# One packed sum for row and offset of an expert slot, index casts on GpSimd, and three expert blocks emitted behind the last head

## The chip, the cores and the metric

The kernel runs on one core of one Trainium2 chip. The metric is the device time of one execution in microseconds. Of the kernel before, three executions gave 1765.59, 1766.91 and 1767.95 us; the median is 1766.91 us. One further execution was profiled; it took 1767.14 us, of which the span from its first to its last instruction is 1765.3 us.

## The reference: what is computed

One layer of an encoder trunk over 512 tokens of 1024 channels, in float32. The first half (attention, a matrix-memory mixer, gates, an output projection) is not touched by the change. The second half is a layer of 16384 single-neuron experts, addressed by product keys, and a final RMSNorm:

```
q = (xb @ w_pq).reshape(PEER_BLOCK, PEER_HEADS, 2, D_KEY // 2)
s = einsum("thpd,hpnd->thpn", q, sub_keys)          # 8 heads, 2 halves, 128 keys
s_top, i_top = top_k(s, 16)
cand = s_top[:, :, 0, :, None] + s_top[:, :, 1, None, :]   # 16 x 16 sums
best, ci = top_k(cand.reshape(..., 256), 16)
i1 = take_along_axis(i_top[:, :, 0, :], ci // 16)
i2 = take_along_axis(i_top[:, :, 1, :], ci % 16)
e = i1 * 128 + i2
gate = softmax(best)
act = gelu(einsum("thkd,td->thk", u_exp[e], xb))
out = einsum("thk,thkd->td", gate * act, v_exp[e])
```

So each token has 8 x 16 = 128 slots, and each slot has a row i1, a column i2 and a gate.

## The kernel before

**Dense experts for three quarters of the tokens.** For the last 384 tokens the kernel doesn't gather: it multiplies the tokens with all 16384 rows of u, in 128 blocks of 128 experts (`hidden`: one load of 512 KB, a split of the weights into a high and a low part, 24 matmuls of 384 columns, one GELU), weights the result with a dense gate matrix, and multiplies with v (`output`). The first 128 tokens gather their rows (`gathered`).

**Split weights.** Every weight tile is split in two halves of 512 columns. `split` lets ScalarE copy a half into a rounded high part `whi` (L150), and VectorE or GpSimd subtract it for the low part `wlo` (L153); in the stages discussed here the halves go to VectorE, GpSimd, GpSimd in turn. Each product is then three matmuls, L163 to L165, and the second operand of L165 needs `wlo`.

**The scores stage.** `scores` runs over eight heads. For a head it projects two queries (`ps_pq`, 2 x 24 matmuls of 512 columns), multiplies with the keys (`ps_sc`), and takes the 16 best of 128 keys, with their places, for four token tiles and two halves (`top16`, L647 to L651 on VectorE). It then calls `select`:

- L656 casts the places of the keys from uint32 to float32 (`idx`), 128 elements a partition.
- Only 50 of the 256 sums can be among the best 16; they lie as a staircase: row a of the staircase has 16 // (a + 1) candidates and begins at `OFFS[a]`. GpSimd forms them (L660, L663), `top16` finds the best 16 and their positions, L668 casts these (`pf`).
- L670 and L671 form `dl`, the differences of neighbouring rows' key indices. L686 forms a mask m over 16 x 16: position >= OFFS[a]. The product m * dl, summed over a, is the key index of the slot's row (L687 on GpSimd, L688 on VectorE, written to `slots`). The product m * (length of the row before), summed over a, is where the row begins (L689 on GpSimd, L690 on VectorE); L691 subtracts it from the position, which gives the offset in the row. L692, L693 and L694 turn the offset into the column's key index.

After the eight heads `scores` forms the gates (L634 to L641).

**The build stage.** For each of three token tiles `build` transposes the slots (`ps_slT`, L739), forms one-hot matrices on three engines (L750, L760, L761, L764) and multiplies them into the dense gate matrix (`ps_g`, L766). It has 32 steps a tile, 96 in all, and stores the matrix to HBM (L772, on GpSimd's queue).

**What sets the order.** `front` is a generator that yields twice for a head, once behind the gates and once for a build step. The loop at L938 to L944 counts these yields with n, adds `RATE_S` = 1.0 to a counter for the first 16 and `RATE_B` = 0.15 for those behind, and emits one block of `hidden` (through `ahead`) whenever the counter reaches one; 40 blocks are to be emitted in this way, and what is left then is emitted in one go by `drive` (L945). This is the order in which instructions are written down. Their order on each engine is made from it when the program is built, by a planner that runs the program in a model of its own and lets an engine take up something later in the text where what comes first isn't ready in that model. On the chip each engine then keeps its order and waits.

Of the kernel before, what the change touches and what calls it, by code (L numbers as in the profile page):

```python
# [10 lines left out]
F32 = mybir.dt.float32  # L11
# [5 lines left out]
ALU = mybir.AluOpType  # L17
AX = mybir.AxisListType
# [3 lines left out]
P = 128  # L22
# [8 lines left out]
TOPK = 16  # L31
STAIR = [TOPK // (a + 1) for a in range(TOPK)]
OFFS = [sum(STAIR[:a]) for a in range(TOPK)]
NC50 = sum(STAIR)
TB = 32
EG = 4
GG = 8
# [9 lines left out]
ADA_AT, ADA_N = 8, 2  # L47
OAP, OAD, TWO = 6, 16, 6
ACT_N, ACT_D = 2, 2
RATE_S, RATE_B, RATE_V = 1.0, 0.15, 2.5  # L50
WST, WB = 4, 5

LANES_A = lambda nc: [nc.vector]
# [3 lines left out]
C_BADA, C_G1, C_G2, C_CW, C_CB, C_MG, C_BG, C_OFF, C_DOFF, C_SEQ = 0, 48, 56, 64, 96, 104, 108, 112, 128, 144  # L57
# [17 lines left out]
def drive(*gens):  # L75
    for _ in weave(*gens):
        pass
# [3 lines left out]
def tile_block(  # L81
# [19 lines left out]
    nc = tc.nc  # L101
# [8 lines left out]
    def bank(tag, name):  # L110
        return psum.tile([P, 512], F32, tag=tag, name=name, bufs=4 if tag == "acc" else 2)
# [13 lines left out]
    cst = cpool.tile([P, C_N], F32, name="cst")  # L125
# [76 lines left out]
    x2d = dram.tile([4, P, D], F32, name="x2d")  # L202
    gd = dram.tile([S // TB, P, P, TB], F32, name="gd")
    gtd = dram.tile([1, D], F32, name="gtd")
# [440 lines left out]
    def top16(vals, places, data):  # L645

        nc.vector.max(vals[:, :8], data)  # L647
        nc.vector.max_index(places[:, :8], vals[:, :8], data)  # L648
        nc.vector.match_replace(data, vals[:, :8], data, LOWEST)  # L649
        nc.vector.max(vals[:, 8:], data)  # L650
        nc.vector.max_index(places[:, 8:], vals[:, 8:], data)  # L651

    def select(cp, h, sv, i16, best, slots):

        idx = cp.tile([P, 4, 2, TOPK], F32, tag="idx", name="idx")
        nc.vector.tensor_copy(idx, i16)  # L656
        cand = cp.tile([P, 4, NC50], F32, tag="cand", name="cand", bufs=1)
        for a in range(8):
            nb = STAIR[a]
            nc.gpsimd.tensor_add(  # L660
                cand[:, :, OFFS[a] : OFFS[a] + nb], sv[:, :, 1, :nb], sv[:, :, 0, a : a + 1].broadcast_to([P, 4, nb])
            )
        nc.gpsimd.tensor_add(cand[:, :, OFFS[8] :], sv[:, :, 0, 8:], sv[:, :, 1, 0:1].broadcast_to([P, 4, 8]))  # L663
        pos = cp.tile([P, 4, TOPK], U32, tag="pos", name="pos")
        for i in range(4):
            top16(best[:, i, h], pos[:, i], cand[:, i])
        pf = cp.tile([P, 4, TOPK], F32, tag="pf", name="pf")
        nc.vector.tensor_copy(pf, pos)  # L668
        dl = cp.tile([P, 4, TOPK], F32, tag="dl", name="dl")
        nc.vector.tensor_copy(dl[:, :, 0:1], idx[:, :, 0, 0:1])  # L670
        nc.vector.tensor_sub(dl[:, :, 1:], idx[:, :, 0, 1:], idx[:, :, 0, :-1])  # L671
        of = cp.tile([P, 4, TOPK], F32, tag="of", name="of")
        shp = [P, 4, TOPK, TOPK]

        def bc(t):
            return t.unsqueeze(3).broadcast_to(shp)

        def bs(t):
            return t.unsqueeze(2).broadcast_to(shp)

        def bq(col):
            return cst[:, col : col + TOPK].unsqueeze(1).unsqueeze(1).broadcast_to(shp)

        m = cp.tile(shp, F32, tag="m4", name="m4", bufs=1)
        q = cp.tile(shp, F32, tag="q4", name="q4", bufs=1)
        nc.vector.tensor_tensor(out=m, in0=bc(pf), in1=bq(C_OFF), op=ALU.is_ge)  # L686
        nc.gpsimd.tensor_mul(q, m, bs(dl))  # L687
        nc.vector.tensor_reduce(slots[:, :, 0, h], q, axis=AX.X, op=ALU.add)  # L688
        nc.gpsimd.tensor_mul(m, m, bq(C_DOFF))  # L689
        nc.vector.tensor_reduce(of, m, axis=AX.X, op=ALU.add)  # L690
        nc.vector.tensor_sub(of, pf, of)  # L691
        nc.vector.tensor_tensor(out=m, in0=bc(of), in1=bq(C_SEQ), op=ALU.is_equal)  # L692
        nc.gpsimd.tensor_mul(m, m, bs(idx[:, :, 1, :]))  # L693
        nc.vector.tensor_reduce(slots[:, :, 1, h], m, axis=AX.X, op=ALU.add)  # L694
# [40 lines left out]
    def build(cp, i, slots):  # L735
# [7 lines left out]
        nc.scalar.mul(neg, sT[:, 1:, :], -1.0)  # L743
        for b in range(P // TB):
            st = cp.tile([P, P, TB], F32, tag="gst", name="gst", bufs=2)
            for t4 in range(TB // 4):
                ps = bank("gw"[t4 % 2], "ps_g")
                o4 = cp.tile([P, 4, P], F32, tag="two", name="o4", bufs=TWO)
                t0 = b * TB + t4 * 4
                mark = nc.vector.tensor_tensor(  # L750
# [3 lines left out]
                for tt in range(4):  # L754
                    t = b * TB + t4 * 4 + tt
                    oa = cp.tile([P, P], F32, tag="oap" if tt == 1 else "oad", name="oa", bufs=OAP if tt == 1 else OAD)
# [19 lines left out]
    def gather_side(cp):  # L776
        for i in range(NG):
            yield from gathered(cp, i)

    def front(sp, dp, h2T):  # L780
        yield from scores(sp, h2T)
        for i in range(NG, 4):
            yield from build(dp, i, state["slots"][:, i])
# [97 lines left out]
    def pool(name, bufs=2, side="left"):  # L881
        return tc.tile_pool(name=name, bufs=bufs, side=side, reuse_waits="tile")
# [45 lines left out]
    with pool("epool") as cp:  # L928
        h2T = state["h2T"]
        held = cp.tile([P, HOLD, ND], F32, name="held", bufs=1)  # L930
        state["slots"] = cp.tile([P, 4, 3, 8, TOPK], F32, name="slots", bufs=1)
        with pool("dpool") as dp, pool("upool") as up:
            gt2 = dp.tile([P, D], F32, tag="m4", name="gt2", bufs=1)
            to_rows(gt2, mod[:, 40:48], 1.0)
            nc.sync.dma_start(gtd, gt2[:1, :])
            main, side = front(dp, dp, h2T), ahead(up, h2T, held)
            lanes["now"] = LANES_F(nc)
            n, due = 0, 0.0  # L938
            for _ in main:
                n += 1  # L940
                due += RATE_S if n <= 16 else RATE_B
                while due >= 1.0:
                    due -= 1.0
                    next(side, None)  # L944
            drive((side, 1))  # L945
            lanes["now"] = LANES_V(nc)
        if stop == "u":
            return
        with pool("vpool") as vp, pool("rpool") as rp:
            gather = gather_side(rp)  # L950
            with tc.issue_after(state["marks"][MARK]):
                next(gather)
                next(gather)
            paced(output(rp, vp, h2T, held), gather, RATE_V)
            drive((gather, 1))


def layout(inputs):
# [23 lines left out]
    consts = np.zeros((P, C_N), np.float32)  # L982
# [6 lines left out]
    consts[:BH, C_BG] = f["b_igate"][0]  # L989
    consts[32 : 32 + BH, C_BG] = f["b_fgate"][0]  # L990
    consts[:, C_OFF : C_OFF + 16] = OFFS
    consts[:, C_DOFF : C_DOFF + 16] = [0] + STAIR[:-1]
    consts[:, C_SEQ : C_SEQ + 16] = np.arange(16)

    dist = 3 * P + np.arange(P)[:, None] - np.arange(512)[None, :]
    return {
# [31 lines left out]
```

## Time and profile before

| | |
|---|---|
| median of three executions | 1766.91 us (1765.59 to 1767.95) |
| the profiled execution | 1767.14 us |
| its span | 1765.3 us |
| TensorE matmul (PE) busy | 1705.3 us, 97% |
| VectorE (DVE) busy | 1380.5 us, 78% |
| GpSimd (POOL) busy | 832.6 us, 47% |
| ScalarE (ACT) busy | 806.3 us, 46% |
| mean DMA rate | 234 GB/s |

In a row of a group, the numbers behind the bar of the count are the busy time in us, the mean duration of one instruction in ns, and the time that its engine sat idle just before such instructions, with what ended it. In a row of a stretch of time stand the busy time of each engine with its count of instructions, the granted TensorE clock as a share of full speed, the busy share of the DMA engines and their rate. In a row of waits stand the total in us, the number of waits and the longest.

### The profile page before, as it was taken

To read this page: it belongs to the slowest core of one execution; us is meant where nothing else is said; L and a number is where in the kernel's file an instruction comes from. 1 tells how busy PE (TensorE), PEld (TensorE's weight loads), DVE (VectorE), ACT (ScalarE), POOL (GpSimd) and SP (SyncE) were. 2 spreads that over 40 slices of the span, in tenths; PEclk is the share of its full clock that TensorE was granted. 3 is DMA by queue.
4 is the path that set the end of the run, shared out by engine and by line. 5 is a ranking of instruction groups with operands and counts; after the bars stand their busy time and mean duration, and the time that the engine had idled before them with its cause. 6 is when DMAs were issued, how large, how long until landed. Compare 5 with 4: busy or idle time off the path is not lost.

```text
span 1765.3 us, 25467 instructions
## 1 busy us (share of the span) xinstructions
PE 1705.3 (97%) x8671; PEld 1486.5 (84%) x8671; DVE 1380.5 (78%) x2868; ACT 806.3 (46%) x1624; POOL 832.6 (47%) x692
## 2 busy tenths in 40 slices
PE   5999999999999897999999999999999999999997
PEld 4766678888798787999899999999999999998886
DVE  7557655675589998899477988899989898898445
ACT  4544545443543334998533443433434443434443
POOL 0000000000157676999455666677776677673221
PEclk9999999999999998999999999999999999999999
DMA  8423224563332333565998989989999989987653
GB/s 292 152 73 127 88 99 140 186 227 100 111 104 89 104 101 135 204 255 233 343 367 322 358 308 344 352 324 342 348 326 351 353 303 351 350 293 282 228 194 107
DMA packets 129940, 413.35 MB, mean 234 GB/s; under 512 B 12049, under 2 KB 38801, under 8 KB 128274
## 3 DMA queue, kind: packets, MB, share of 16 engines
q1 hardware_dynamic: 91218, 252.33, 41.3%
q0 software_dynamic: 38592, 159.40, 24.1%
q8 instruction: 68, 1.11, 0.2%
q14 instruction: 62, 0.51, 0.1%
HBM read 376.03 MB, written 35.66 MB: 233 GB/s over the span
## 4 chain that ended last, share of the span: by engine, by line
PE 80%; DVE 13%; DMA 4%; issue 1%; POOL 1%; ACT 1%; SPq 0%; DVEq 0%; ACTq 0%
PE acc L165 10%; PE acc L164 10%; PE acc L163 10%; PE ps_act L165 8%; PE ps_act L163 8%; PE ps_act L164 8%; PE ps_g L766 4%; DVE wlo L153 2%; DMA wst<-in_w_ada 1%; PE ps_ya L361 1%; PE ps_s L341 1%; PE ps_qk L163 1%; DVE i L648 1%; PE ps_qk L165 1%; DVE sc L649 1%
## 5 line engine op out<-in xcount | busy, mean ns | idle before, releaser
L150 ACT CAST whi<-wst 128x512 fp32r<-128x512 f32 x408 | 252.1, 621 | 482.6 <-PE ps_act L164 279.6
L165 PE MATMUL ps_act<-h2T_hi,wlo 128*128 128x384 f32 x1024 | 348.3, 340 | 5.0 <-DVE wlo L153 4.0
L163 PE MATMUL ps_act<-h2T_hi,whi 128*128 128x384 f32 x1024 | 347.0, 339 | 0.0
L164 PE MATMUL ps_act<-h2T_lo,whi 128*128 128x384 f32 x1024 | 346.8, 339 | 0.0
L164 PE MATMUL acc<-wlo,ehi 128*128 128x512 f32 x768 | 299.1, 391 | 0.0
L163 PE MATMUL acc<-whi,ehi 128*128 128x512 f32 x768 | 293.3, 390 | 3.3 <-ACT whi L150 3.3
L165 PE MATMUL acc<-whi,elo 128*128 128x512 f32 x768 | 286.9, 391 | 0.0
L153 DVE TENSOR_TENSOR wlo<-wst,whi 128x512 fp32r<-128x512 f32 x275 | 207.0, 756 | 98.2 <-ACT whi L150 91.1
L153 POOL TENSOR_TENSOR wlo<-wst,whi 128x512 fp32r<-128x512 f32 x133 | 184.4, 1393 | 180.9 <-ACT whi L150 174.9
L150 ACT CAST whi<-vst 128x512 fp32r<-128x512 f32 x256 | 158.0, 620 | 181.2 <-PE acc L165 137.9
L724 POOL DMA_INDIRECT vr<-in_v_r,ei x128 | 168.6, 1317 | 84.5 <-DVE sum_v L730 65.9
L710 POOL DMA_INDIRECT ur<-in_u_r,ei x128 | 153.5, 1199 | 115.3 <-DVE junk L713 93.6
L153 POOL TENSOR_TENSOR wlo<-vst,whi 128x512 fp32r<-128x512 f32 x85 | 131.0, 1541 | 151.7 <-ACT whi L150 136.1
L165 PEld LDWEIGHTS ps_act<-h2T_hi,wlo 128*128 128x128 f32 x1024 | 193.8, 189 | 7.3 <-DVE wlo L153 5.2
L163 PEld LDWEIGHTS ps_act<-h2T_hi,whi 128*128 128x128 f32 x1024 | 194.0, 189 | 3.7
L164 PEld LDWEIGHTS ps_act<-h2T_lo,whi 128*128 128x128 f32 x1024 | 193.9, 189 | 3.7
L730 DVE SCALAR_TENSOR_TENSOR sum_v<-vr,act,sum_v 128x1024 f32<-128x1024 f32 x127 | 181.2, 1427 | 1.2 <-DMA vr<-in_v_r,ei 0.4
L713 DVE SCALAR_TENSOR_TENSOR junk<-ur,h 128x1024 bf16<-128x1024 f32 x128 | 170.9, 1335 | 0.9
L163 PEld LDWEIGHTS acc<-whi,ehi 128*128 128x128 f32 x768 | 144.6, 188 | 31.5 <-ACT whi L150 3.6
L165 PEld LDWEIGHTS acc<-whi,elo 128*128 128x128 f32 x768 | 144.0, 188 | 30.4 <-DVE elo L841 0.2
L164 PEld LDWEIGHTS acc<-wlo,ehi 128*128 128x128 f32 x768 | 144.1, 188 | 28.5
L471 POOL TENSOR_SCALAR_AFFINE_SELECT mbd<-mbc 128x512 f32<-128x512 f32 x4 | 4.7, 1163 | 319.5 <-ACT mbc L469 319.5
(300 smaller groups left out, 3103.8 us busy)
## 6 DMA issues: line engine op xcount, KB each, us to landing
wst<-in_u_t SPq DMA_DIRECT2D x128, 512.0 KB
vst<-in_v_e SPq DMA_DIRECT2D x128, 512.0 KB
wst<-in_w_pieces SPq DMA_DIRECT2D x76, 512.0 KB
wst<-in_w_ada SPq DMA_DIRECT2D x48, 512.0 KB
gd<-gst POOLq DMA_DIRECT2D x12, 2048.0 KB
gq<-gd SPq DMA_DIRECT2D x16, 1536.0 KB
ad<-gelu SPq DMA_DIRECT2D x8, 768.0 KB
aq<-ad SPq DMA_DIRECT2D x8, 768.0 KB
```

What stands on the lines that cost most here:

```text
L150: nc.scalar.copy(hi, t[:, cs])
L153: e.tensor_tensor(out=lo, in0=t[:, cs], in1=hi.bitcast(F32), op=ALU.subtract)
L163: nc.tensor.matmul(o, a[0], b[0], start=first, stop=False)
L164: nc.tensor.matmul(o, a[0], b[1], start=False, stop=False)
L165: return nc.tensor.matmul(o, a[1], b[0], start=False, stop=last)
L341: nc.tensor.matmul(pss[:, :n], qaT[po : po + 64, cs], kaT[po : po + 64, hp, :n], start=True, stop=True)
L361: nc.tensor.matmul(psy[po : po + 64, cs], va[:, kt, h * 64 : (h + 1) * 64], pt[:, kt * P : (kt + 1) * P], start=kt == 0, stop=kt == qt,)
L710: nc.gpsimd.indirect_dma_start(out=t, out_offset=None, in_=u_r, in_offset=bass.IndirectOffsetOnAxis(ap=ei[:, j : j + 1], axis=0))
L713: nc.vector.scalar_tensor_tensor(junk(), t, 1.0, state["h2"][i], op0=ALU.mult, op1=ALU.mult, accum_out=act[:, j : j + 1])
L724: nc.gpsimd.indirect_dma_start(out=t, out_offset=None, in_=v_r, in_offset=bass.IndirectOffsetOnAxis(ap=ei[:, j : j + 1], axis=0))
L730: nc.vector.scalar_tensor_tensor(sum_v, t, act[:, j : j + 1], sum_v, op0=ALU.mult, op1=ALU.add)
L766: nc.tensor.matmul(ps[:, tt::4], oa, ob, start=True, stop=True)
```

## The change

The two sums over the mask become one: `dl` is scaled by 64 and the length of the row before is added to it, so the sum over a holds 64 times the key index plus the row's beginning (less 24, a bias that keeps the remainder within half of 64). Adding and subtracting 1.5 * 2^23 rounds the quotient to a whole number; the remainder gives the offset. The product L689 and the reduction L690 go; five small instructions on 64 elements a partition come. The two casts and the copy of four elements (L656, L668, L670) move from VectorE to GpSimd. At the seventeenth yield, the one behind the gates, three blocks of `hidden` are emitted, and 0.14 of a block for each build step.

```diff
+PACK, BIAS, WHOLE = 64, 24, 1.5 * 2.0**23
...
-RATE_S, RATE_B, RATE_V = 1.0, 0.15, 2.5
+RATE_S, TOP, RATE_B, RATE_V = 1.0, 3.0, 0.14, 2.5
...
         idx = cp.tile([P, 4, 2, TOPK], F32, tag="idx", name="idx")
-        nc.vector.tensor_copy(idx, i16)
+        nc.gpsimd.tensor_copy(idx, i16)
...
         pf = cp.tile([P, 4, TOPK], F32, tag="pf", name="pf")
-        nc.vector.tensor_copy(pf, pos)
+        nc.gpsimd.tensor_copy(pf, pos)
         dl = cp.tile([P, 4, TOPK], F32, tag="dl", name="dl")
-        nc.vector.tensor_copy(dl[:, :, 0:1], idx[:, :, 0, 0:1])
+        nc.gpsimd.tensor_copy(dl[:, :, 0:1], idx[:, :, 0, 0:1])
         nc.vector.tensor_sub(dl[:, :, 1:], idx[:, :, 0, 1:], idx[:, :, 0, :-1])
+        nc.vector.scalar_tensor_tensor(
+            dl, dl, float(PACK), cst[:, C_DOFF : C_DOFF + TOPK].unsqueeze(1).broadcast_to([P, 4, TOPK]),
+            op0=ALU.mult, op1=ALU.add,
+        )
...
         nc.gpsimd.tensor_mul(q, m, bs(dl))
-        nc.vector.tensor_reduce(slots[:, :, 0, h], q, axis=AX.X, op=ALU.add)
-        nc.gpsimd.tensor_mul(m, m, bq(C_DOFF))
-        nc.vector.tensor_reduce(of, m, axis=AX.X, op=ALU.add)
-        nc.vector.tensor_sub(of, pf, of)
+        both = cp.tile([P, 4, TOPK], F32, tag="both", name="both")
+        nc.vector.tensor_reduce(both, q, axis=AX.X, op=ALU.add)
+        nc.vector.tensor_scalar(of, both, 1.0 / PACK, WHOLE, op0=ALU.mult, op1=ALU.add)
+        nc.vector.tensor_scalar_add(slots[:, :, 0, h], of, -WHOLE)
+        nc.vector.scalar_tensor_tensor(of, slots[:, :, 0, h], float(PACK), both, op0=ALU.mult, op1=ALU.subtract)
+        nc.vector.tensor_add(of, of, pf)
...
-                due += RATE_S if n <= 16 else RATE_B
+                due += RATE_S if n <= 16 else TOP if n == 17 else RATE_B
...
-    consts[:, C_DOFF : C_DOFF + 16] = [0] + STAIR[:-1]
-    consts[:, C_SEQ : C_SEQ + 16] = np.arange(16)
+    consts[:, C_DOFF : C_DOFF + 16] = [-BIAS] + STAIR[:-1]
+    consts[:, C_SEQ : C_SEQ + 16] = BIAS + np.arange(16)
```

## The prediction

> **What bounds the kernel now.** I read the head of the page first, then the busy times of the engines in stretches of time, then TensorE's waits, then the instruction groups of the two engines that the change touches.
>
> ```profile
> span 1765.3 us, 25467 instructions
> PE 1705.3 (97%) x8671; PEld 1486.5 (84%) x8671; DVE 1380.5 (78%) x2868; ACT 806.3 (46%) x1624; POOL 832.6 (47%) x692
> ```
>
> TensorE is busy for 97% of the span, and the change leaves its matmuls as they are. So a gain can only come from what is left of TensorE: 1765.3 - 1705.3 = 60.0 us idle, and time in which it runs at a lower clock. The stretches show where the change could reach it: six heads of the scores stage, each from the first `ps_pq` of a head to that of the next (the sixth up to the end of the two `hidden` blocks behind it), and then the stretch up to the first `ps_g` of the build stage.
>
> ```profile
> 512.06:533.12 21.06, 21.06 (x114) 19.15 (x113) 20.99 (x98) 7.90 (x14) 17.29 (x18) 1.00 0.33 106
> 533.12:554.17 21.05, 21.05 (x113) 19.14 (x113) 20.98 (x94) 7.90 (x14) 14.75 (x16) 1.00 0.23 79
> 554.17:576.42 22.25, 21.71 (x114) 18.99 (x113) 22.15 (x108) 7.89 (x14) 15.51 (x17) 1.00 0.30 98
> 576.42:600.77 24.35, 21.83 (x113) 18.96 (x113) 24.24 (x108) 7.89 (x14) 15.98 (x17) 1.00 0.30 97
> 600.77:626.20 25.43, 22.54 (x114) 18.80 (x113) 25.22 (x114) 7.89 (x14) 17.41 (x19) 1.00 0.37 120
> 626.20:651.05 24.85, 22.77 (x111) 19.65 (x111) 24.78 (x108) 7.89 (x14) 16.84 (x17) 0.93 0.23 70
> 651.05:704.88 53.83, 42.32 (x219) 41.01 (x219) 46.28 (x148) 22.26 (x47) 38.48 (x31) 0.87 0.38 128
> ```
>
> The columns behind the length are PE, PEld, DVE, ACT and POOL. The same 113 or so matmuls take 21.06 us in the first two heads, with TensorE full, and 22.25 to 25.43 us in the next four, where it is VectorE that is full (24.24 of 24.35 us). VectorE is full in the first two heads as well; what it does not get done there it carries along. Against 21.06 us the four heads lose 1.19 + 3.29 + 4.37 + 3.79 = 12.6 us. TensorE's waits from 497 to 704 us name the same engine:
>
> ```profile
> PE ps_slT L739 <- DVE slots L688: 7.5, 1, 7.5
> PE ps_act L165 <- DVE wlo L153: 4.0, 4, 2.5
> PE ps_pq L165 <- DVE wlo L153: 3.6, 3, 1.9
> PE ps_pq L165 <- POOL wlo L153: 3.3, 4, 1.8
> PE ps_act L165 <- POOL wlo L153: 0.9, 1, 0.9
> ```
>
> These are 19.3 us: 11.8 us for low parts of weights, late in the queues of VectorE and GpSimd, and 7.5 us for the slots of the last head. What is due to the clock follows from the pace of a block:
>
> ```profile
> 670.44 0.34 PE L163 MATMUL ps_act<-h2T_hi,whi 128*128 128x384 f32 x1
> ...
> 678.25 0.34 PE L163 MATMUL ps_act<-h2T_hi,whi 128*128 128x384 f32 x1
> 686.10 0.48 PE L739 MATMUL ps_slT<-ident,slots 128*128 128x128 f32 x1 [7.51 <-DVE slots L688]
> 686.23 0.67 PE L164 MATMUL ps_act<-h2T_lo,whi 128*128 128x384 f32 x1
> ```
>
> Between the first two of these rows lie 45 steps, so a matmul of 384 columns takes 7.81 / 45 = 0.174 us and a block of 24 takes 4.17 us. The 219 matmuls of the last stretch are nearly all of this kind, which is 38.0 us of its 53.83: it loses 15.8 us, to waits and to a clock of 0.87. The most that the change can win is thus 12.6 + 15.8 us, and 3.3 us more from a place shown below.
>
> **The two sums made one, and the casts moved.** VectorE's groups in six heads, 512 to 651 us:
>
> ```profile
> L690 DVE TENSOR_REDUCE of<-m 128x64 f32<-128x1024 f32 x6 | 7.2, 1200 | 0.0
> L656 DVE CAST idx<-i 128x128 f32<-128x128 uint32 x6 | 6.4, 1072 | 0.1
> ...
> L670 DVE COPY dl<-idx 128x4 f32<-128x4 f32 x6 | 3.3, 556 | 0.1
> ...
> L691 DVE TENSOR_TENSOR of<-pf,of 128x64 f32<-128x64 f32 x6 | 2.4, 403 | 0.0
> ...
> L668 DVE CAST pf<-pos 128x64 f32<-128x64 uint32 x6 | 1.2, 193 | 0.2
> ```
>
> From VectorE go, in a head, 1.200 + 1.072 + 0.556 + 0.403 + 0.193 = 3.42 us. Five instructions of 64 elements come, which this trace does not show. L691 is nearest, the same size with two tensor inputs: 5 x 0.403 = 2.0 us. The bounds are the cheapest and the dearest small row, L668 and L670: 0.97 and 2.78 us. VectorE saves 1.4 us a head, between 0.6 and 2.5. On GpSimd:
>
> ```profile
> L153 POOL TENSOR_TENSOR wlo<-wst,whi 128x512 fp32r<-128x512 f32 x31 | 41.9, 1364 | 0.0
> L689 POOL TENSOR_TENSOR m<-m,cst 128x1024 f32<-128x1024 f32 x6 | 15.6, 2602 | 0.2
> L687 POOL TENSOR_TENSOR q<-m,dl 128x1024 f32<-128x1024 f32 x6 | 14.8, 2466 | 25.9 <-DVE m L686 25.9
> L693 POOL TENSOR_TENSOR m<-m,idx 128x1024 f32<-128x1024 f32 x6 | 14.8, 2462 | 12.1 <-DVE m L692 7.1 <-PE ps_pq L164 2.9 <-PE ps_act L164 2.0
> L660 POOL TENSOR_TENSOR cand<-v 128x8 f32<-128x8 f32 (+5 forms) x48 | 10.9, 258 | 3.0 <-DVE v L647 2.8 <-DVE v L650 0.2
> ```
>
> L689 goes, 2.60 us a head. Three small instructions come. As small additions (L660) they cost 3 x 0.258 = 0.8 us. The dearest row of that size is in the build stage, from 705 to 846 us:
>
> ```profile
> L764 POOL TENSOR_SCALAR oa<-iota,sT 128x128 f32<-128x128 f32 x93 | 103.4, 1122 | 0.6
> ```
>
> By that one they cost 3.4 us. I take 0.8, since the two smaller ones have 64 and 4 elements; GpSimd then has 1.8 us less a head, and 0.8 us more at worst. It is busy for 14.8 to 17.4 us of a head of 21.06, so it is no bound either way.
>
> What hides the casts is GpSimd's idle time: it waited 25.9 us in six heads for the mask of L686, 4.3 us each, and `pf` is needed just ahead of that mask. If this cover is gone, the wait falls on VectorE (third rival).
>
> **What this is worth on TensorE.** In the heads: 1.4 us times the four slow heads is 5.6 us, times all six, with the backlog of the first two, 8.4. I take 7; bounds 4 x 0.6 = 2.4 and all 12.6. In the stretch behind them, the backlog with which the last `select` starts shrinks only by what VectorE gains beyond what TensorE gains, and the last head saves its own 1.4 us and a reduction's turn behind GpSimd. The 7.5 us wait for L688 is one of order: the transpose stands in TensorE's queue ahead of a block whose matmuls follow 0.13 us behind it (686.23). I take 6 of the 15.8 us: most of that one wait, or parts of several. Bounds 0 and 14. What is late next are low parts of weights for the blocks that fill this stretch.
>
> At this place a rule of the Trainium skill speaks against the change. First the rows, of all eight heads, durations as least, median and greatest:
>
> ```profile
> L656 DVE CAST idx<-i x8: 211/700/1965, 502.8 to 668.1; 128x128 f32<-128x128 uint32 x8
> L688 DVE TENSOR_REDUCE slots<-q x8: 1193/1204/1212, 515.5 to 684.8; 128x64 f32<-128x1024 f32 x8
> ```
>
> The same cast takes 211 or 1965 ns, while a reduction keeps within 19 ns. The Trainium skill's page "SBUF — State Buffer", section "Who interferes with whom", says that VectorE and GpSimd share a port pair as an exclusive lock, that copies, casts, tensor-scalar instructions and those with two SBUF inputs can take it and the later one waits, and that a reduction never contends on trn2. The two rows agree. By this rule the change takes out a reduction that never waited and puts in five instructions that can; that is the first rival.
>
> **The three blocks and the rate.** Each block moved is one load of 512 KB on SP's queue, two casts and a GELU on ScalarE, two subtractions, 24 matmuls, and for every fourth a store on SP's queue. The text emits 16 blocks in the heads and, with 97 x 0.15 = 14, thirty by the last build step; after the change 16 + 3 + 13 = 32, and `drive` has 8 instead of 10. On TensorE the trace is far ahead of the text. The two rows count the first matmul form (8 a block) up to 686 us and up to 846.2 us:
>
> ```profile
> L163 PE MATMUL ps_act<-h2T_hi,whi 128*128 128x384 f32 x168 | 57.4, 342 | 0.0
> ```
> ```profile
> L163 PE MATMUL ps_act<-h2T_hi,whi 128*128 128x384 f32 x302 | 104.5, 346 | 0.0
> ```
>
> That is 21 blocks ahead of the transpose, where the text has 16, and 37.8 at the end of the build, where it has 30. Blocks 17 to 19 were taken up early already, so their new place changes nothing that I can see: 0. The DMA engines are at a share of 0.38 there, so the earlier loads on SP's queue collide with little. Bounds: it could win the wait of 7.5 us, which lies in the stretch above, or cost cover at the end of the build:
>
> ```profile
> 846.16:875.00 28.84, 25.57 (x150) 25.25 (x148) 6.98 (x14) 10.92 (x21) 11.53 (x11) 1.00 0.93 340
> ```
> ```profile
> PE acc L163 <- ACT whi L150: 3.3, 1, 3.3
> ```
>
> From the last `ps_g` to the first matmul with v pass 28.84 us, and blocks cover 25.57 of them; then TensorE waits 3.3 us. If the heads end earlier, fewer blocks will have been used up as filling and a little more cover is left: I take 1 us won. Bounds 3.3 won, and 12.5 us (three blocks of 4.17) lost.
>
> **Sum.** 7 + 6 + 1 = 14 us from the profiled execution's 1767.1 us (its span and 1.8 us around it) gives 1753. That execution lies 0.2 us above the median shown. By the bounds without the loss of cover: 1737 to 1765.
>
> **Rivals.**
> *The port gives it back.* If each added instruction costs what the dearest small row does (2.78 us) VectorE saves 0.6 us a head: 2.4 us in the slow heads, and some 2.5 us behind them, 1762 us. For it: L656 stretched from 211 to a mean of 1072 ns. Against: GpSimd loses 2.6 us a head of the very work that does the stretching. This is the result that the rule above would give.
> *Cover lost at the build's end.* Three blocks less between 846 and 875 us cost 12.5 us: 1767.1 - 13 + 12.5 = 1766.6, no change. For it: the stretch is covered to within 3.3 us now. Against: the lead of 7.8 blocks shows that emission does not set how many are done.
> *VectorE waits for the cast: slower.* `pf` now comes from GpSimd, whose queue may hold the product L693 of the head before (2.46 us) and one L153 (1.36 us) ahead of the cast (0.26 us): 4.1 us in which VectorE's queue stands at L686, with the next head's `top16` and its share of `wlo` behind it, and TensorE behind these. Less the 1.4 us saved this is 2.7 us a head, 21 us in eight: 1788. It decides from a mean wait of 1.4 us. Against it: the 4.3 us for which GpSimd idles a head just there.
> *It changes nothing*: TensorE is full again at once, and the order of the planner puts new waits in the place of the old; 1767.
>
> **How the numbers follow.** Forecast 0.55, port 0.15, cover 0.12, cast 0.10, nothing 0.08. About 0.2%, 3.5 us, is what a measurement of this kernel can tell from no change. Nearly all of the forecast (0.52), two thirds of the port (0.10) and a part of cover and nothing (0.06) are faster by more: 0.68. The cast, and a fourth of cover and of nothing, are slower with a stray of the rest: 0.16. The remaining 0.16 is the same. The range goes from 1738 to 1767; what is left out is the cast, the worse half of lost cover and a tail below. The forecast's own is 1740 to 1762.
>
> **What would show it.** Right: the four slow heads come down to about 22.5 us each, waits for `wlo` from 11.8 us to 6 or less, the wait at `ps_slT` shorter, a clock near 1.00 from 626 us on, GpSimd's idle time before L687 shorter by the cast but VectorE's before the mask near 0. Wrong: small new rows of 0.5 us and above (port), a wait above 3.3 us before the first `acc` (cover), VectorE idle until GpSimd's `pf` (cast).

## The result, and the profile after

The changed kernel takes 1751.95 us, the median of four executions (1746.61 to 1753.08). The kernel before, beside it on the same chip, takes 1766.25 us (1764.48 to 1767.95). The ratio is 0.991, with a 95% interval from 0.9888 to 0.9931: 14.3 us or 0.8% less. The profiled execution took 1752.6 us, and its span is 14.5 us shorter than the one before. These are the head and the engines of its page:

```profile
span 1750.8 us, 25492 instructions
...
PE 1700.3 (97%) x8671; PEld 1485.4 (85%) x8671; DVE 1356.2 (77%) x2868; ACT 807.3 (46%) x1624; POOL 818.1 (47%) x708
```

TensorE's idle time fell from 60.0 us to 1750.8 - 1700.3 = 50.5 us. VectorE is busy for 24.3 us less, GpSimd for 14.5 us less. Where the time went is seen in the same stretches as before: six heads, the stretch from there to the first `ps_g`, and, last, the stretch from the last `ps_g` to the first matmul with v.

```profile
595.47:616.52 21.05, 21.05 (x113) 19.14 (x113) 20.02 (x101) 7.90 (x14) 14.23 (x21) 1.00 0.46 144
616.52:638.15 21.63, 21.51 (x114) 19.23 (x114) 21.06 (x114) 8.03 (x15) 15.21 (x19) 1.00 0.30 102
638.15:683.76 45.61, 38.17 (x206) 36.16 (x205) 39.95 (x141) 21.71 (x46) 34.97 (x33) 0.96 0.42 139
824.26:859.36 35.10, 29.03 (x169) 28.71 (x167) 7.67 (x15) 12.49 (x24) 12.78 (x12) 0.99 0.94 342
```

The slow heads are gone: the first five heads take 21.05 or 21.06 us with TensorE full (the fifth is shown), the sixth 21.63. The six together went from 138.99 us to 126.89, which is 12.1 us less. The next stretch went from 53.83 us to 45.61. Its 13 fewer matmuls are work done elsewhere (13 x 0.174 = 2.3 us); 5.9 us are time no longer lost. The last stretch went from 28.84 us to 35.10: 3.5 us of this is TensorE's own work on 19 more matmuls, and 2.8 us is a longer wait. What is left (the first of the six heads starts 0.8 us earlier, the build is 0.8 us shorter, all behind the first matmul with v is 1.1 us longer) nearly cancels against the 3.5 - 2.3 us of moved work.

TensorE's waits from 640 to 860 us, in total, number and longest:

```profile
PE acc L164 <- ACT whi L151: 6.1, 1, 6.1
PE ps_slT L746 <- DVE slots L696: 5.1, 1, 5.1
PE ps_act L166 <- POOL wlo L154: 1.8, 3, 1.3
...
PE ps_act L166 <- DVE wlo L154: 0.5, 1, 0.5
```

From 497 to 704 us, the window in which the kernel before waited 11.8 us for low parts and 7.5 us for the slots, only the second, third and fourth of these occur: 2.3 us for low parts and 5.1 us for the slots. The first, at v, has grown from 3.3 us.

VectorE's groups in the six heads, 511 to 638 us. The line numbers are higher by one ahead of the new lines, and by five or more behind them:

```profile
L154 DVE TENSOR_TENSOR wlo<-wst,whi 128x512 fp32r<-128x512 f32 x15 | 13.0, 867 | 0.0
...
L691 DVE TENSOR_TENSOR m<-pf,cst 128x1024 f32<-128x1024 f32 x6 | 9.5, 1579 | 0.7 <-POOL pf L669 0.7
L699 DVE TENSOR_TENSOR m<-of,cst 128x1024 f32<-128x1024 f32 x6 | 7.8, 1297 | 0.0
...
L673 DVE SCALAR_TENSOR_TENSOR dl<-dl,cst 128x64 f32<-128x64 f32 x6 | 3.4, 562 | 0.1
...
L695 DVE TENSOR_SCALAR of<-both 128x64 f32<-128x64 f32 x6 | 2.5, 416 | 0.0
L672 DVE TENSOR_TENSOR dl<-idx 128x60 f32<-128x60 f32 x6 | 2.4, 392 | 0.0
...
L698 DVE TENSOR_TENSOR of<-of,pf 128x64 f32<-128x64 f32 x6 | 1.4, 229 | 0.0
L696 DVE TENSOR_SCALAR slots<-of 128x64 f32<-128x64 f32 x6 | 1.4, 227 | 0.0
L697 DVE SCALAR_TENSOR_TENSOR of<-slots,both 128x64 f32<-128x64 f32 x6 | 1.2, 203 | 0.0
```

Four rows of the kernel before, from its six heads, answer to the first three of these and to L672:

```profile
L153 DVE TENSOR_TENSOR wlo<-wst,whi 128x512 fp32r<-128x512 f32 x15 | 21.3, 1420 | 0.0
...
L686 DVE TENSOR_TENSOR m<-pf,cst 128x1024 f32<-128x1024 f32 x6 | 7.3, 1223 | 0.2
L692 DVE TENSOR_TENSOR m<-of,cst 128x1024 f32<-128x1024 f32 x6 | 7.2, 1206 | 0.0
...
L671 DVE TENSOR_TENSOR dl<-idx 128x60 f32<-128x60 f32 x6 | 1.3, 209 | 0.0
```

The rows account for VectorE. What the change takes out was 6 x 3.42 = 20.5 us. The five added groups cost 3.4 + 2.5 + 1.4 + 1.4 + 1.2 = 9.9 us, 1.64 us a head. Low parts of weights, which the change doesn't touch, cost 21.3 - 13.0 = 8.3 us less; the two masks and L672 cost 3.9 us more. Together that is 15.0 us saved; the windows show VectorE busy for 138.37 us before and 123.92 us after, 14.5 us less. The moved instructions on GpSimd, in the same window:

```profile
L671 POOL COPY dl<-idx 128x4 f32<-128x4 f32 x6 | 2.4, 402 | 0.3
L657 POOL CAST idx<-i 128x128 f32<-128x128 uint32 x6 | 2.2, 367 | 1.4 <-DVE i L652 1.4
L669 POOL CAST pf<-pos 128x64 f32<-128x64 uint32 x6 | 1.5, 244 | 4.8 <-DVE pos L652 4.7
```

They cost 6.1 us in six heads, 1.01 us each. VectorE's wait for `pf` is 0.7 us in six heads.

### The profile page after: what moved, and what is told of

Read it like the earlier page. It is cut to its first block, busy times and chain, and to the rows that moved or that the text cites. A ratio compares the mean times of both kernels' runs of the same rounds, so it can differ in the third digit from the quotient of the medians.

```text
span 1750.8 us, 25492 instructions
## 1 busy us (share of the span) xinstructions
PE 1700.3 (97%) x8671; PEld 1485.4 (85%) x8671; DVE 1356.2 (77%) x2868; ACT 807.3 (46%) x1624; POOL 818.1 (47%) x708
## 3 DMA queue, kind: packets, MB, share of 16 engines
q0 software_dynamic: 38592, 159.40, 24.4%
## 4 chain that ended last, share of the span: by engine, by line
PE 80%; DVE 12%; DMA 4%; issue 1%; POOL 1%; ACT 1%; SPq 0%; DVEq 0%; POOLq 0%; ACTq 0%
PE acc L165 10%; PE acc L164 10%; PE acc L166 10%; PE ps_act L164 8%; PE ps_act L165 8%; PE ps_act L166 8%; PE ps_g L773 3%; DMA wst<-in_w_ada 2%; DVE wlo L154 1%; DVE oa L771 1%; PE ps_ya L362 1%; PE ps_s L342 1%; DMA vst<-in_v_e 1%; DVE o L757 1%; DMA wst<-in_w_pieces 1%
## 5 line engine op out<-in xcount | busy, mean ns | idle before, releaser
L154 DVE TENSOR_TENSOR wlo<-wst,whi 128x512 fp32r<-128x512 f32 x275 | 195.2, 712 | 103.1 <-ACT whi L151 96.4
L731 POOL DMA_INDIRECT vr<-in_v_r,ei x128 | 161.0, 1258 | 89.3 <-DVE sum_v L737 70.0
L154 DVE TENSOR_TENSOR wlo<-vst,whi 128x512 fp32r<-128x512 f32 x171 | 132.5, 776 | 29.1 <-ACT whi L151 29.0
```

The lines of the kernel that those rows point to most:

```text
L154: e.tensor_tensor(out=lo, in0=t[:, cs], in1=hi.bitcast(F32), op=ALU.subtract)
L731: nc.gpsimd.indirect_dma_start(out=t, out_offset=None, in_=v_r, in_offset=bass.IndirectOffsetOnAxis(ap=ei[:, j : j + 1], axis=0))
```

## The experiments

Two theories were set against each other: that TensorE gets what VectorE's own instructions no longer take (in the expectations, VectorE's time), and that it gets what VectorE no longer loses behind GpSimd's work (the port, by the name of the prediction's first rival). "Six heads" is always the time from the third `ps_pq` head to the end of the second `hidden` block behind the eighth: 139.0 us before, 126.9 us after; the windows end within four matmuls (0.7 us) of one another. The floor, with TensorE full, is 6 x 21.05 = 126.3 us. The ratios go against the kernel before on the same chip.

| kernel | median, us | ratio | 95% interval | six heads, us |
|---|---|---|---|---|
| packed sum alone | 1764.79 | 0.9978 | 0.9963 to 0.9994 | 136.95 |
| casts and copy on GpSimd alone | 1767.51 | 1.0005 | 0.9985 to 1.0024 | 139.43 |
| pace alone | 1768.88 | 1.0009 | 0.9993 to 1.0025 | 139.2 |
| after, with two of three casts and copy back on VectorE | 1758.60 | 0.9946 | 0.9927 to 0.9965 | 132.45 |
| after, one more GpSimd product a head | 1765.96 | 0.9997 | 0.998 to 1.0014 | 138.19 |
| after, one more VectorE reduction a head | 1762.74 | 0.997 | 0.9956 to 0.9984 | 136.34 |
| before, without the product L689 | 1765.79 | 0.9995 | 0.9982 to 1.0008 | 140.54 |
| before, without the reduction L690 | 1766.78 | 0.9998 | 0.9984 to 1.0012 | 134.54 |
| after, gather queued later | 1748.97 | 0.9896 | 0.987 to 0.9922 | 126.4 |
| after, six blocks behind the last head | 1747.56 | 0.989 | 0.9863 to 0.9916 | 126.4 |
| after, once more | 1752.23 | 0.9917 | 0.9892 to 0.9942 | 126.6 |
| after, gather later and six blocks | 1746.33 | 0.9883 | 0.9858 to 0.9908 | 126.6 |

### The packed sum alone

```diff
+        nc.vector.scalar_tensor_tensor(dl, dl, float(PACK), ...)
-        nc.vector.tensor_reduce(slots[:, :, 0, h], q, axis=AX.X, op=ALU.add)
-        nc.gpsimd.tensor_mul(m, m, bq(C_DOFF))
-        nc.vector.tensor_reduce(of, m, axis=AX.X, op=ALU.add)
-        nc.vector.tensor_sub(of, pf, of)
+        nc.vector.tensor_reduce(both, q, axis=AX.X, op=ALU.add)
...
+        nc.vector.tensor_add(of, of, pf)
```

> The packed sum alone; casts and copy stay on VectorE, blocks emitted as before. Theory A (the gain is VectorE's own instruction time in a head): the reduction and the subtraction that go (1.60 us a head in the profile of before) are about paid for by the five small instructions that come (1.63 us a head in the profile of after), so no gain: 1763 to 1770 us, slow heads still near 24 us. Theory B (the gain is the port: GpSimd loses a product of 2.6 us a head, and VectorE's instructions with two inputs wait less behind it): most of the gain is here: 1752 to 1758 us, the mean of a low part on VectorE falls from 1.42 us to under 1.0.

It won 0.2%. The time is in the range of theory A, and the low parts do what theory B said. The stretch of its six heads, and two groups in it:

```profile
513.35:650.30 136.95, 128.55 (x672) 114.08 (x672) 132.32 (x650) 47.37 (x84) 84.94 (x97) 1.00 0.30 97
```
```profile
L154 DVE TENSOR_TENSOR wlo<-wst,whi 128x512 fp32r<-128x512 f32 x15 | 14.2, 944 | 0.0
...
L694 DVE TENSOR_REDUCE both<-q 128x64 f32<-128x1024 f32 x6 | 7.3, 1209 | 4.0 <-POOL q L692 4.0
```

GpSimd has 12.8 us less than the 97.78 us of before, and the low parts on VectorE take 944 ns instead of 1420. Still the heads are only 2.0 us shorter: VectorE has 4.6 us of idle time now, and 4.0 of it is a wait for the product `q` that the kernel before did not have. It comes from the planner's order. In the kernel before, 21 to 29 other instructions of VectorE, 3.4 to 6.0 us of work, stand between the mask (L686) and the reduction of `q` each time; here only 4 to 9, 0.8 to 1.9 us, stand ahead of the last three of the six reductions, and VectorE idles for 1.0 to 1.7 us before each. The two casts and the copy are still on VectorE.

### The casts and the copy alone

```diff
-        nc.vector.tensor_copy(idx, i16)
+        nc.gpsimd.tensor_copy(idx, i16)
...
-        nc.vector.tensor_copy(pf, pos)
+        nc.gpsimd.tensor_copy(pf, pos)
...
-        nc.vector.tensor_copy(dl[:, :, 0:1], idx[:, :, 0, 0:1])
+        nc.gpsimd.tensor_copy(dl[:, :, 0:1], idx[:, :, 0, 0:1])
```

> The two casts and the copy on GpSimd alone; the two sums and the emission as before. Theory A: VectorE saves 1.82 us a head (1.072 + 0.556 + 0.193), heads fall to about 22.5 us: 1753 to 1758 us. Theory B: GpSimd gets 1.0 us a head more and loses nothing, so VectorE's low parts keep waiting (1.3 us and more): 1760 to 1766 us.

No difference can be measured; 1767.51 us lies above the ranges of both theories. The six heads and three groups of VectorE that changed:

```profile
509.87:649.30 139.43, 129.89 (x672) 115.26 (x672) 136.11 (x611) 47.39 (x84) 105.32 (x121) 0.99 0.30 95
```
```profile
L153 DVE TENSOR_TENSOR wlo<-wst,whi 128x512 fp32r<-128x512 f32 x16 | 24.3, 1521 | 0.0
...
L686 DVE TENSOR_TENSOR m<-pf,cst 128x1024 f32<-128x1024 f32 x6 | 9.5, 1577 | 1.3 <-POOL pf L668 1.0
...
L671 DVE TENSOR_TENSOR dl<-idx 128x60 f32<-128x60 f32 x6 | 4.3, 712 | 0.0
```

From VectorE went 1.82 us a head, 10.9 us in six. These three groups alone took back 16 x 0.10 + 6 x 0.35 + 6 x 0.50 = 6.7 us in longer instructions, and 1.3 us in the wait before the mask, most of it for `pf`; GpSimd is busy for 7.5 us more. So for this part alone the freed time is given back, as the rival of the port has it; the planner's order of VectorE and GpSimd is new here too. By the rule of the Trainium skill's page "SBUF — State Buffer", section "Who interferes with whom", that the prediction weighed, VectorE's instructions with two SBUF inputs contend with GpSimd's that read SBUF, and a reduction on VectorE never does on trn2. This trace agrees: the means of its three reductions are 1194 to 1200 ns, while the low parts on VectorE, from 500 to 690 us, spread like this (least, median and greatest in ns):

```profile
L153 DVE TENSOR_TENSOR wlo<-wst,whi x21: 661/760/2723, 509.0 to 684.2; 128x512 fp32r<-128x512 f32 x21
```

### The pace alone

```diff
-RATE_S, RATE_B, RATE_V = 1.0, 0.15, 2.5
+RATE_S, TOP, RATE_B, RATE_V = 1.0, 3.0, 0.14, 2.5
-                due += RATE_S if n <= 16 else RATE_B
+                due += RATE_S if n <= 16 else TOP if n == 17 else RATE_B
```

> Three blocks behind the last head and 0.14 a build step alone. As forecast, the new places move nothing, since TensorE's order is ahead of the text: 1764 to 1768 us. Theory C (the pacing carries part of the gain): 1758 to 1763 us, and a shorter wait at the transposed slots.

No difference can be measured (1768.88 us is just above the range), and there is none to find: the order of the instructions on all five engines is the same as in the kernel before.

### Two of the three moved instructions put back

```diff
-        nc.gpsimd.tensor_copy(pf, pos)
+        nc.vector.tensor_copy(pf, pos)
...
-        nc.gpsimd.tensor_copy(dl[:, :, 0:1], idx[:, :, 0, 0:1])
+        nc.vector.tensor_copy(dl[:, :, 0:1], idx[:, :, 0, 0:1])
```

> The changed kernel with the cast of the positions and the copy of four elements back on VectorE; only the large cast is on GpSimd. If one instruction carries the gain of the moved casts (the large one, 1.07 us of the 1.82 us in the profile of before): heads stay near 21.1 to 21.5 us, 1751 to 1756 us. If the gain is a threshold that VectorE passes only with all parts together: heads at 22 us and more, 1757 to 1764 us.

Here only the cast of `idx` is on GpSimd, beside the packed sum. It lies between: 0.5% faster than before, and with 132.45 us in the heads 5.6 us behind the changed kernel. So two of the three moved instructions, where all three together won nothing without the packed sum, are worth 6 to 7 us with it (1758.60 against 1751.95 and 1752.23 us; by the ratios 5 to 6 us). The time is in the range given for a threshold, but about half of the gain is there without all parts together. TensorE's longest waits in these heads are for low parts on GpSimd:

```profile
PE ps_pq L166 <- POOL wlo L154: 5.1, 3, 2.4
```

Ahead of the two longest, the low part stands behind the product `q` in GpSimd's queue, and GpSimd had been idle for 4.9 and 5.0 us until VectorE finished the mask (L691). So these waits for GpSimd go back to VectorE.

### Load put back on one engine at a time

One more product of 1024 elements a partition on GpSimd, whose result nobody uses, behind the packed sum:

```diff
         nc.vector.tensor_reduce(both, q, axis=AX.X, op=ALU.add)
+        nc.gpsimd.tensor_mul(q, q, q)
```

> The changed kernel with one more product of 1024 elements a partition on GpSimd in each head (q times q, not used), some 2.5 us; VectorE's instructions as in the changed kernel. Theory A: GpSimd has room, 1752 to 1755 us. Theory B: VectorE waits behind GpSimd as before, low parts on it back to 1.2 us and above, 1757 to 1763 us.

The whole gain is gone, more than theory B said, though the low parts on VectorE stay below its 1.2 us. VectorE's own instructions are those of the changed kernel; two groups of its six heads, the added product, and one place where the two meet:

```profile
L154 DVE TENSOR_TENSOR wlo<-wst,whi 128x512 fp32r<-128x512 f32 x15 | 15.2, 1013 | 0.0
...
L696 DVE TENSOR_SCALAR of<-both 128x64 f32<-128x64 f32 x6 | 7.7, 1277 | 0.0
```
```profile
L695 POOL TENSOR_TENSOR q<-q 128x1024 f32<-128x1024 f32 x6 | 11.4, 1896 | 2.7 <-DVE both L694 2.6
```
```profile
606.55 1.89 POOL L695 TENSOR_TENSOR q<-q 128x1024 f32<-128x1024 f32 x1 [0.27 <-DVE both L694]
607.23 1.26 DVE L696 TENSOR_SCALAR of<-both 128x64 f32<-128x64 f32 x1
```

L696, on 64 elements, takes 1277 ns on average instead of 416, and between 306 and 3167. In each of the six heads it ends 0.05 or 0.06 us behind an instruction of GpSimd that it overlaps: the added product in four, a low part in two. TensorE's waits from 497 to 704 us name low parts on GpSimd for 9.6 us and on VectorE for 1.7. So the added product delays GpSimd's own queue as well, and this run does not tell the two ways apart. One reduction more a head on VectorE instead:

```diff
         nc.vector.tensor_reduce(both, q, axis=AX.X, op=ALU.add)
+        nc.vector.tensor_reduce(again, q, axis=AX.X, op=ALU.add)
```

> The changed kernel with one more reduction of the same product on VectorE in each head (1.20 us, not used); a reduction kept within 19 ns in the profile of before, so it brings no wait behind GpSimd. If VectorE's time in a head is what decides, whatever it consists of: it had 0.0 to 1.0 us to spare in a head of 21.05, so heads come to 21.8 to 22.5 us, and the time to 1756 to 1761 us. If only waits behind GpSimd decide: heads stay at 21.1 us, 1751 to 1754 us.

Two thirds of the gain are gone, though GpSimd has the changed kernel's work; the time lies just above the range of the first reading. Its heads and groups:

```profile
515.56:651.90 136.34, 129.96 (x673) 115.34 (x672) 135.79 (x632) 47.36 (x84) 91.35 (x116) 0.99 0.31 100
```
```profile
L154 DVE TENSOR_TENSOR wlo<-wst,whi 128x512 fp32r<-128x512 f32 x15 | 15.9, 1061 | 0.0
...
L696 DVE TENSOR_REDUCE again<-q 128x64 f32<-128x1024 f32 x6 | 7.2, 1208 | 0.0
```

7.2 us of reductions made the heads 9.5 us longer. The low parts took 15 x 0.19 = 2.9 us more, without one more instruction on GpSimd. So what VectorE loses behind GpSimd is no amount that GpSimd's load alone sets; the order of both engines, which the planner made anew, has its part in it.

### Load taken from one engine at a time

The kernel before without the product L689, and then without the reduction L690. Their outputs leave a part out, as the expectations say.

```diff
-        nc.gpsimd.tensor_mul(m, m, bq(C_DOFF))
```

> The kernel before without GpSimd's product L689; the reduction L690 then sums the bare mask, so the offset and with it the column of a slot are left out. VectorE's instructions stay. If GpSimd's 2.6 us a head were enough by themselves: heads at 21.5 us or less, 1752 to 1757 us. If it takes both engines: heads at 22.5 us and more, 1759 to 1765 us.

```diff
-        nc.vector.tensor_reduce(of, m, axis=AX.X, op=ALU.add)
-        nc.vector.tensor_sub(of, pf, of)
+        nc.vector.tensor_sub(of, pf, pf)
```

> The kernel before without VectorE's reduction L690; the offset is then zero for every slot, so the right column is left out. GpSimd's instructions stay. By the 1.2 us a head alone, six heads fall from 139 to 132 us: 1758 to 1762 us. If waits behind GpSimd fall with it, as they rose when a reduction was added to the changed kernel (9.8 us in six heads for 7.2 us added): 1754 to 1758 us. If they take its place: 1763 to 1767 us.

Neither makes a difference that can be measured: without the product the time lies just above the range for "it takes both engines", without the reduction in the range for waits that take its place. Without the product, six heads and the next stretch, and the stretch from the last `ps_g` to v:

```profile
511.26:651.80 140.54, 130.11 (x673) 115.23 (x672) 139.99 (x630) 47.40 (x84) 86.62 (x99) 0.99 0.30 97
651.80:691.50 39.70, 32.66 (x175) 31.16 (x175) 38.88 (x139) 21.64 (x43) 27.86 (x25) 0.91 0.45 146
834.20:873.40 39.20, 34.99 (x202) 34.67 (x200) 8.36 (x16) 14.74 (x28) 15.40 (x14) 0.99 0.87 322
```

GpSimd has 11.2 us less, VectorE stays full (139.99 of 140.54 us), and the heads win nothing. The shorter stretch behind them holds 44 matmuls less than before (175 against 219), and the one before v 52 more (202 against 150): most of that was moved, not won. Without the reduction, the heads, and the group that follows the product on VectorE:

```profile
514.86:649.40 134.54, 128.76 (x673) 113.98 (x673) 125.23 (x622) 47.37 (x84) 99.53 (x103) 1.00 0.30 99
```
```profile
L688 DVE TENSOR_REDUCE slots<-q 128x64 f32<-128x1024 f32 x6 | 7.3, 1209 | 7.0 <-POOL q L687 7.0
```

VectorE is busy for 13.1 us less, and 7.0 us of this turn into waits for the product `q`. They come from the order again: ahead of the last three reductions of `q` only one or two instructions of VectorE, 0.1 to 0.7 us, stand behind the mask, and it idles for 2.3 or 2.4 us before each. The heads win 4.5 us, which the median doesn't show. The build (143.8 us against 141.3) and the stretch before v (32.1 against 28.8) are longer; whether that is the new order or this one execution stays open.

### The two waits that are left

The wait at v is one for a transfer. The chain of waits of the changed kernel and of the one before gives the load of the first tile of v from issue to landing. SyncE's timeline of the changed kernel shows the load of gates (L830) that stands ahead of it, and GpSimd's timeline of the kernel before the start of the gather of `u` rows:

```profile
842.07 16.54 DMA vst<-in_v_e
```
```profile
860.51 13.74 DMA vst<-in_v_e
```
```profile
841.63 0.38 SPq L830 DMA_DIRECT2D gq<-gd  x1
```
```profile
861.96 1.04 POOL L710 DMA_INDIRECT ur<-in_u_r,ei  x1 [8.09 <-DVE ei L705]
```

The load goes out 842.07 - 824.26 = 17.8 us after the last `ps_g`, where it was 860.51 - 846.16 = 14.4 us before, since it stands in SyncE's queue behind the loads and stores of the blocks, of which more are left. That is 3.4 us more, about the 3.5 us of added cover. And the load takes 2.8 us longer. At 843.52 us, 1.4 us behind this load, GpSimd begins to issue the gather; the DMA engines' busy share in the stretch is 0.94. In the kernel before the gather begins just as close behind the load, so its presence does not explain the difference between the two. Two experiments took one wait each, a third both. The gather's index computation, and so its loads, queued behind VectorE's low part of the first v tile:

```diff
-            with tc.issue_after(state["marks"][MARK]):
+            main = output(rp, vp, h2T, held)
+            next(main)
+            with tc.issue_after(state["low"].ins):
...
-            paced(output(rp, vp, h2T, held), gather, RATE_V)
+            paced(main, gather, RATE_V)
```

> The changed kernel, with the first indirect loads of the gathered tokens held back until VectorE has made a low part of the first v block (the two instructions that make the list of rows are queued behind it). If the wait of 6.1 us before the first matmul with v comes from the 3 MB of these loads sharing the DMA engines with v and with the gate matrix: the wait falls to 0 to 2 us, 1746 to 1749 us. If it comes from when SP's queue gets to those loads: the wait stays at 5 to 6 us, 1751 to 1753 us.

The stretch from the last `ps_g` to v, and the first load of the gather in GpSimd's timeline:

```profile
825.98:855.94 29.96, 29.86 (x174) 29.54 (x172) 6.83 (x12) 12.42 (x24) 7.07 (x6) 1.00 0.93 335
```
```profile
862.04 1.17 POOL L719 DMA_INDIRECT ur<-in_u_r,ei  x1 [0.16 <-DMA aq<-ad]
```

The first load goes out at 862.04 instead of 843.52 us, and TensorE is full up to v: 174 matmuls in 29.96 us where the changed kernel needs 35.10 us for 169. The load of v lands after 10.86 us. Behind the first matmuls with v a new wait of 2.0 us comes, for a low part on GpSimd that takes 3.98 us. The edit also makes the planner put six more matmuls of blocks ahead of v, 1.0 us of cover. By its median it is 3 us ahead of the changed kernel (1748.01 to 1751.57); the executions and the intervals overlap. The transposed slots next:

```diff
-RATE_S, TOP, RATE_B, RATE_V = 1.0, 3.0, 0.14, 2.5
+RATE_S, TOP, RATE_B, RATE_V = 1.0, 6.0, 0.11, 2.5
```

> The changed kernel with six blocks behind the last head and 0.11 a build step. The order differs from the changed kernel's in one thing: the first transpose of the slots stands one block (24 matmuls) later in TensorE's queue. If the wait of 5.1 us there is one of order alone: it falls to 0 to 2 us, and the time by 2 to 4 us, to 1748 to 1750 us. If the block behind it waits for its own low parts: the wait moves to that block, 1751 to 1753 us.

Only TensorE's order changes by this: the first transpose of slots stands one block, 24 matmuls, later. TensorE's waits from 497 to 704 us:

```profile
PE ps_act L166 <- POOL wlo L154: 3.1, 4, 1.3
PE ps_act L166 <- DVE wlo L154: 1.4, 2, 0.8
PE ps_slT L746 <- DVE slots L701: 1.3, 1, 1.3
```

The wait for the slots falls from 5.1 to 1.3 us; 2.2 us of it come back as waits for low parts. So the wait was, for the larger part, one of order. The median, just below the range of the first reading, is 4.4 us below the changed kernel's; the executions overlap (1745.89 to 1749.91). The changed kernel again, unchanged, on the chip on which both edits were tried together:

> The changed kernel once more, beside the next kernel on the same chip: 1748 to 1754 us.

In this execution the load of v took 14.27 us and TensorE waited 3.8 us for it. So the wait grew by 2.8 us in one execution and by 0.5 us in the other. In the run with the pace alone, whose order is that of the kernel before, the load took 12.43 us and the wait was 2.6 us. So the length of this load differs by 1.3 to 2.3 us between executions of one order. Both edits together:

> The changed kernel with both: the gather's first loads held back, and six blocks behind the last head with 0.11 a build step. If the two places are independent, the gains add: 5 us at the first matmul with v and 2 to 3 us at the transposed slots, 1743 to 1747 us. If blocks used up earlier lay the wait at v open again: 1747 to 1750 us.

```profile
PE acc L167 <- POOL wlo L154: 2.0, 1, 2.0
PE ps_slT L748 <- DVE slots L703: 1.3, 1, 1.3
PE acc L166 <- ACT whi L151: 0.8, 1, 0.8
```

Both waits are short (the first row is the new wait behind the first matmuls with v), and at 1746.33 us (1744.42 to 1748.08) all four executions are faster than each of the changed kernel's beside them (1749.72 to 1753.36). This version is the fastest of the study, 1.2% ahead of the kernel before.

## Why the prediction was right, and where not

**The sum.** 1753 us were forecast, 1751.95 measured; the sum of 14 us stands against 14.5 us of span. Two of its three terms were off, in opposite directions: 5 us too little in the heads, some 4 us too much before v. That the sum is right to half a microsecond is luck.

**VectorE's saving: too small, by a term set at nothing.** The added instructions cost 1.64 us a head, the forecast had 2.0, so the edits save 1.78 instead of 1.4 us. What the step lacked is what VectorE's other instructions gain or lose: 8.3 us won in low parts, 3.9 us lost in masks and differences, 4.4 us net in six heads. VectorE saved 14.5 us in six heads, where 8.4 was the most that the step allowed for with 1.4 us a head.

**The heads: 7 forecast, 12.1 measured.** The step had the place and the mechanism right: VectorE's backlog. Its size came near the upper bound, 12.6 us, all that the slow heads lost. The four heads did not come down to 22.5 us each but to 21.05 to 21.63. The linear price (1.4 us times four heads, or six) was the mistake. In the kernels above that won little, the first one or two of these heads run at TensorE's pace and most later ones are slow (with the packed sum alone, the first five take 21.1, 21.1, 23.6, 23.7 and 24.4 us), which would fit a queue of VectorE that falls behind by a little in each; in the changed kernel no head is slow. Each part alone won 2 us or nothing in the heads (136.95 and 139.43 us), all together 12.1 us.

**The stretch behind the heads: 6 forecast, 5.9 measured.** The waits for low parts in the window of the prediction fell from 11.8 to 2.3 us (6 or less was announced), the one for the slots from 7.5 to 5.1 us. So the term has its size, but it came from parts of several waits; "most of that one wait" did not come true. That the wait for the slots is one of order was borne out by moving the transpose by a block. The clock, announced near 1.00 from 626 us on, is 1.00 in the last two heads and 0.96 in the stretch.

**The gap before v: 1 us won forecast, 2.8 us more wait measured.** "A little more cover is left" was right: 169 matmuls stand there, not 150. The step failed on the load of v, which it left out: its issue moves with the last block's loads and stores in SyncE's queue. The cover grew by 3.5 us and the load went out 3.4 us later, so nothing was won; the 2.8 us on top are the longer load, and in a second execution they were 0.5. Why this load takes longer in one execution than in another stays open. With the gather issued later the wait before the first matmul with v was gone, and 2.0 us came back behind it.

**The blocks and the rate at 0:** right; added to the kernel before, they leave the order of instructions as it was.

**The casts: hidden, as forecast.** They cost GpSimd 1.01 us a head (0.8 forecast), and VectorE waited 0.7 us in six heads for `pf`. The rival in which VectorE waits for the cast, which needed a mean wait of 1.4 us, is out.

**The port.** Its sign, new rows of 0.5 us and above, showed in one of five rows (L673, 562 ns). As a rival for the whole change it was wrong by 10 us (1762 against 1751.95). The argument held against it, that GpSimd loses 2.6 us of product a head, is supported by the run in which a product put back takes the whole gain away. For the casts alone it was right: VectorE's longer instructions and its waits give most of the freed 10.9 us back.

**What is shown and what isn't.** Shown: the pace does nothing; the parts alone win 0.2% or nothing; a product put back on GpSimd takes the gain away and a reduction put back on VectorE two thirds of it (0.9997, 0.997); and taking either out of the kernel before gives nothing (0.9995, 0.9998), with the order that the planner then makes. TensorE's order is no rival in the heads: its first 3003 matmuls, up to 658 us and later, come in one order in all these kernels. With the packed sum alone its whole order is the changed kernel's, but for the first transpose, which stands two matmuls later. What differs in the heads is the load and the order of VectorE and GpSimd, and these two were not separated: the waits for `q` above (4.0 and 7.0 us) come from VectorE's order. So it is not shown that VectorE's saved time would not do alone in a better order. That VectorE's queue, its waits on GpSimd included, has to stay within 21.05 us a head is the reading that fits these kernels; it was not varied in small steps. In the stretch behind the heads TensorE's order differs too.

## What to carry to other kernels

Where a queue falls behind the bottleneck engine by little per round, don't price an edit as its own time times the rounds: much of the freed time can come back as other waits until the queue keeps up, and several parts that measure as little alone may be worth more than their sum (2.0 us and nothing in the heads here, 12.1 together, and about half of that in a kernel between). When a part alone wins nothing, look whether the planner gave it an order with new waits. Count the busy time of both VectorE and GpSimd, with the stretching of untouched instructions as a term of its own (the mean against the shortest of a group shows how much there is). And where cover moves, look up in the queues what the covered load is issued behind and what other transfers it shares the DMA engines with.

## What the runs showed of the hardware that had not been expected

- A tensor-scalar instruction on 64 elements a partition took 416 ns on average in the changed kernel and 1277 ns with one more GpSimd product a head; there it ended 0.05 or 0.06 us behind a GpSimd instruction in all six heads. The means of the reductions of 1024 elements stayed at 1.19 to 1.21 us in every kernel.
- The mask of 1024 elements (L686 before, L691 after) took 1223 ns on average in the kernel before, and 1396 to 1608 ns in the four kernels of the heads' experiments in which GpSimd casts `pf`. The longer mean is that of one or two masks in six: where a low part on GpSimd had begun 0.07 to 0.12 us ahead of it the mask took 2.28 to 2.32 us and ended 1.1 us behind that low part; the others took 1.20 to 1.23 us, but for one of 1.40. Where the mask began 0.02 us first (658.30 us in the changed kernel) it took 1.21 us, and the low part on GpSimd 2.33.
- A reduction added to VectorE, with nothing added to GpSimd, raised the mean of the low parts from 867 to 1061 ns, in an order of its own.
